# A two-layer block in one kernel: a longer stretch of one-chunk weight lookahead at the end of three matrix products

## The chip, the cores and the metric

The kernel runs on one core of a Trainium2 chip. The time is device time in microseconds (us) of one execution. A core has a matmul engine (TensorE, in the profile PE, its weight loads PEld), a vector engine (VectorE, DVE), an activation engine (ScalarE, ACT), GpSimd (POOL) and a sync engine (SP) that here only issues DMA transfers.

## The reference, cut to what matters

The input is 256 tokens of width 1024 in fp32. A first block of two layers runs, then a second one. The places of the change are in the first block:

```python
# layer 1 mixer (GLA): x @ w_in is cut into q, k, v, r, a; then a decayed state over 4 chunks of tokens
o = group_norm(o) * o_norm
m = (o * silu(r)) @ w_o                                # "gwo"
x = layer_norm(ALPHA * x + m)
x = layer_norm(ALPHA * x + conv_ffn(x))                # "up1" and "dn1"; "up0", "dn0" in layer 0
gate = sigmoid(x @ ple_w_gate[i] + ple_b_gate[i])      # "gate0" (layer 0), "gate1" (layer 1)
x = x + gate * (p[i] @ ple_w_proj[i])                  # "pa", "pb"
```

After layer 0's gate comes the GLA mixer, whose first product is "gv0". After layer 1's gate comes the second block, whose first product is "f10", a SwiGLU.

## The kernel before, in words

All weights stream from HBM in the order of use, in 556 chunks of 128x1024 fp32 (512 KB); one chunk is eight 128x128 blocks, and blocks are numbered through the whole program. Every product is done in three matmuls per block, `mm3` (lines 406 to 408): weight high half times activation high half, weight high half times activation low half, weight low half times activation high half. So each chunk has to be split before use. ScalarE writes the high half (`wh`, line 316), VectorE the low half (`wl = wraw - wh`, line 318). Both halves have eight buffers, the raw chunks six.

The class `Stream` decides where in the program these two instructions stand, and since each engine works through its instructions in program order, this is also their order in time. Whenever TensorE's code takes its first block of a new chunk c, `take` issues the preparation of further chunks: up to c + 7, but at most two at a time, when nothing else is said; up to c + 1 when `W.lazy` is 1. The low half has a rule of its own: it isn't issued with its high half but with the next chunk's preparation, or when the chunk in use is the last one prepared:

```python
la = self.lazy or min(self.LA, max(min(c, 3), c // 4))
if c >= self.np or c != self.last:
    self.prep_upto(max(c, min(c + la, self.np + 1)))
if c >= self.np - 1:
    self.flush()
```

`gemm_t` sets `W.lazy` to 1 for the last TAIL[name] blocks of a product that is called with `lazy=True` (ten where the table has no entry). The first group of a product that follows a layer norm always runs with lookahead 1, with single extra preparations (`W.fill`) at fixed steps of it. A group is two columns of blocks (four in a first group) whose results leave PSUM together.

The three products in question:

- "gate0", blocks 888 to 951, chunks 111 to 118: a first group of 32 blocks under the layer norm, then two groups of 16 blocks, chunks 115 and 116, 117 and 118. Behind each group `gate_evac` takes the sigmoid (ScalarE, line 1140), multiplies by `PP` (line 1141: VectorE, but GpSimd for columns 2 and 3) and adds to X (VectorE, line 1143). During the last group `gate_hook` splits the new X column by column into XH and XL (`xsplit`, lines 506 and 507), columns 0 to 5 before that group's steps 1 to 6. Columns 6 and 7 follow behind the last group, then a split of `ph`; then "gv0" begins with chunk 119 (its matmuls are lines 411 to 413).
- "gate1", blocks 1756 to 1819, chunks 219 to 227, built alike; "f10" follows, taking chunk 227 in its first step (lines 466 to 469) and chunk 228 in its second.
- "gwo", blocks 1148 to 1211, chunks 143 to 151: three groups of two columns, then two of one. Its evacuation (`LN.evac`, lines 571 to 595) adds each group to X and gathers the layer norm's sums, on VectorE (line 579 is the addition that frees the PSUM tile), ScalarE and GpSimd. "pa1" (one chunk of work, two groups) follows, then "up1" from block 1220, whose first group, under the layer norm, ends in chunk 156. The convolution behind each later group of "up1" is VectorE work, too (lines 1115 and 1116).

Of the kernel before, what the change touches and what calls it, by code (L numbers as in the profile page):

```python
# [144 lines left out]

TAIL = {"": 10, "gate0": 18, "gate1": 21, "aq": 24, "wo": 0, "cout": 14, "ao": 14}
LOOK = {"": 1, "aq": 2}

LN_AT = {"": (1, 2, 4), "early": (0, 1, 3)}
# [72 lines left out]
def block_kernel(ctx: ExitStack, tc: tile.TileContext, wd, xin, pin, pos, vecs, con1, con2, wa2, fb, out):  # L224
# [190 lines left out]
    def gemm_t(name, xs, T, evac, hook=None, lazy=False, ln=None, to=None, small=False, dst=None, first=False):  # L415
# [12 lines left out]
        for gi, g in enumerate(groups):  # L428
# [12 lines left out]
            for kc in range(nk):  # L441
# [4 lines left out]
                if to and base == 2 and kc == nk // 2:  # L446
                    to.mid()
                W.lazy = 1 if raw else LOOK.get(name, LOOK[""]) if lazy and W.pos >= end - TAIL.get(name, TAIL[""]) else 0
                xh, xl = ln.raw(kc) if raw else xs(kc)
# [1147 lines left out]
```

## Time and profile before

| | us |
|---|---|
| median of 3 runs | 1748.02 (1742.68 to 1754.02) |
| the profiled execution | 1743.21, of it 1741.4 span |
| TensorE busy | 1703.5 |
| VectorE busy | 1210.9 |
| ScalarE busy | 997.3 |
| GpSimd busy | 218.2 |
| mean granted TensorE clock | 0.992 |

The span is the time from the first to the last instruction of one execution. An engine's busy time is the sum of its instructions; where an instruction waited, the profile names the engine and line that released it. The granted clock is the share of full speed that TensorE was given: 1.0 or 0.5.

### The profile page before, as it was taken

The page shows a single profiled execution, that of the slowest core. Times are in us where ns is not written, and L with a number is a line of the kernel's source. Part 1 is how long each engine was busy: PE and PEld are TensorE (multiplying, and loading weights), DVE is VectorE, ACT ScalarE, POOL GpSimd, SP SyncE. Part 2 cuts the span into 40 slices and gives each one's busy share as a digit, 9 for nine tenths or more (in the row PEclk, how much of TensorE's full clock was granted, in tenths as well). Part 3 has the DMA queues.
Part 4 walks back from the last instruction along what each step waited for, and adds up shares of the span by engine and source line. Part 5 has one row for each costly group of instructions (what it writes and reads, how often), then busy time and mean ns, then how long its engine had stood idle before and what let it go on. Part 6 is the DMA issues. An engine that isn't in the chain of part 4 may idle for free.

```text
span 1741.4 us, 34304 instructions
## 1 busy us (share of the span) xinstructions
PE 1703.5 (98%) x13954; PEld 1669.3 (96%) x13954; DVE 1210.9 (70%) x1951; ACT 997.3 (57%) x1575; POOL 218.2 (13%) x244
## 2 busy tenths in 40 slices
PE   7999999999999999999999999999999999999997
PEld 6999999997899999999999999999999999999997
DVE  5777898766689986765557777556755556787553
ACT  5666766556467665654445546445555545766542
POOL 6100311020003210200002020000200001120002
PEclk9999999999999999999999999999999999999999
DMA  6445466635444665375553736554456665147651
GB/s 225 133 135 166 137 215 209 194 124 213 145 141 152 217 198 187 120 246 171 180 182 114 226 110 220 181 181 159 159 167 194 194 194 187 62 146 254 194 182 37
DMA packets 82991, 298.18 MB, mean 171 GB/s; under 512 B 9320, under 2 KB 10488, under 8 KB 82833
## 3 DMA queue, kind: packets, MB, share of 16 engines
q1 hardware_dynamic: 82176, 294.13, 52.2%
q0 software_dynamic: 656, 1.87, 0.4%
q8 instruction: 109, 1.79, 0.4%
q14 instruction: 50, 0.40, 0.1%
HBM read 294.91 MB, written 1.05 MB: 170 GB/s over the span
## 4 chain that ended last, share of the span: by engine, by line
PE 64%; DVE 3%; issue 1%; POOL 1%; ACT 0%; POOLq 0%; DVEq 0%; ACTq 0%
PE acc L406 20%; PE acc L408 20%; PE acc L407 20%; DVE wl L318 1%; DVE XL L565 0%; PE aux L645 0%; PE acc L466 0%; PE acc L469 0%; PE aux L1455 0%; PE acc L467 0%; POOL X L700 0%; PE aux L408 0%; PE aux L406 0%; PE aux L407 0%; PE aux L1478 0%
## 5 line engine op out<-in xcount | busy, mean ns | idle before, releaser
L316 ACT ACTIVATE wh<-wraw 128x1024 fp32r<-128x1024 f32 (+1 forms) x557 | 579.1, 1055 | 352.4 <-PE acc L407 297.2
L406 PE MATMUL acc<-XH,wh 128*128 128x256 f32 (+3 forms) x2660 | 749.2, 282 | 3.0 <-DVE cv L1116 2.5
L408 PE MATMUL acc<-XH,wl 128*128 128x256 f32 (+3 forms) x2660 | 746.2, 281 | 1.0 <-DVE wl L318 1.0
L407 PE MATMUL acc<-XL,wh 128*128 128x256 f32 (+3 forms) x2660 | 745.8, 280 | 0.0
L318 DVE TENSOR_TENSOR wl<-wraw,wh 128x1024 fp32r<-128x1024 f32 (+1 forms) x557 | 678.5, 1248 | 69.0 <-ACT wh L316 65.0
L406 PEld LDWEIGHTS acc<-XH,wh 128*128 128x128 f32 x2660 | 501.4, 188 | 4.1 <-ACT wh L316 1.9
L408 PEld LDWEIGHTS acc<-XH,wl 128*128 128x128 f32 x2660 | 501.1, 188 | 1.8 <-DVE wl L318 1.8
L407 PEld LDWEIGHTS acc<-XL,wh 128*128 128x128 f32 x2660 | 501.4, 188 | 0.0
L406 PE MATMUL acc<-hs,wh 128*128 128x256 f32 (+1 forms) x1044 | 292.4, 280 | 0.0
L408 PE MATMUL acc<-hs,wl 128*128 128x256 f32 (+1 forms) x1044 | 291.2, 279 | 0.0
L407 PE MATMUL acc<-hs,wh 128*128 128x256 f32 (+1 forms) x1044 | 291.2, 279 | 0.0
L407 PEld LDWEIGHTS acc<-hs,wh 128*128 128x128 f32 x1044 | 196.2, 188 | 0.2
L406 PEld LDWEIGHTS acc<-hs,wh 128*128 128x128 f32 x1044 | 196.2, 188 | 0.2
L408 PEld LDWEIGHTS acc<-hs,wl 128*128 128x128 f32 x1044 | 196.2, 188 | 0.0
L1314 DVE SCALAR_TENSOR_TENSOR sg<-acc,sg 128x272 f32<-128x272 f32 (+1 forms) x84 | 36.2, 432 | 185.3 <-ACT sg L1313 185.3
L587 POOL TENSOR_TENSOR ln_q<-ln_w 128x512 f32<-128x512 f32 (+1 forms) x10 | 14.2, 1425 | 974.5 <-ACT ln_w L581 974.5
L581 ACT ACTIVATE ln_w<-X 128x512 f32<-128x512 f32 (+3 forms) x40 | 21.3, 533 | 92.4 <-DVE X L579 92.3
L1121 POOL TENSOR_TENSOR gl<-cv,gl 128x256 f32<-128x256 f32 x44 | 39.8, 905 | 185.0 <-ACT gl L1120 105.9
L579 DVE TENSOR_TENSOR X<-acc,X 128x512 f32<-128x512 f32 (+3 forms) x40 | 22.4, 561 | 56.4 <-PE acc L408 56.2
L1313 ACT ACTIVATE sg<-acc 128x272 f32<-128x272 f32 (+1 forms) x84 | 32.5, 389 | 47.1 <-PE acc L408 46.5
L1113 ACT ACTIVATE cv<-acc,vec 128x256 f32<-128x256 f32 x80 | 40.6, 558 | 28.7 <-PE acc L408 28.6
L565 DVE SCALAR_TENSOR_TENSOR XL<-X,vec,XH 128x256 fp32r<-128x256 f32 (+1 forms) x72 | 53.9, 778 | 3.4 <-ACT XH L564 3.4
(418 smaller groups left out, 2275.8 us busy)
## 6 DMA issues: line engine op xcount, KB each, us to landing
wraw<-wd SPq DMA_DIRECT2D x555, 512.0 KB, 4.3
X<-xin SPq DMA_DIRECT2D x4, 272.0 KB, 6.2
out_t<-X SPq DMA_DIRECT2D x3, 256.0 KB, 2.7
wraw<-wd SPq DMA_DIRECT2D x2, 256.0 KB, 4.0
praw<-pin POOLq DMA_DIRECT2D x2, 256.0 KB, 3.0
fpt<-con POOLq DMA_DIRECT2D x2, 256.0 KB, 3.0
cum<-con POOLq DMA_DIRECT2D x1, 408.0 KB, 4.1
vec<-vecs SPq DMA_DIRECT2D x1, 283.0 KB, 7.6
```

The source lines that it names most:

```text
L316: A.activation(h[:, k], r[:, k], AF.Copy)
L318: self.low = lambda h=h, l=l, r=r, i=i: [V.tensor_tensor(l[:, k], r[:, k], f32(h[:, k]), op=SUB) for k in self.cuts(i)]
L406: mm(o, wh, xh, start=start, stop=False)
L407: mm(o, wh, xl, start=False, stop=False)
L408: mm(o, wl, xh, start=False, stop=stop)
L565: V.scalar_tensor_tensor(l, self.x1(m), vc(self.g, self.j + m), f32(h), op0=MUL, op1=SUB)
L579: V.tensor_tensor(xv, psum, xv, op=ADD)
L581: A.activation(sq, xv, AF.Square)
L1113: A.activation(t[:, e, :], psum[:, e, :], AF.Identity, scale=cw(2, e, j), bias=vc("cb", i * 44 + e * 22 + j))
L1121: G.tensor_tensor(gl, t[:, 0, :], gl, op=MUL)
L1313: A.activation(s, psum[:, 0, :], AF.Silu)
L1314: V.scalar_tensor_tensor(s, psum[:, 1, :], 0.5, s, op0=MUL, op1=MUL)
```

## The change

The table of tails gets an entry for "gwo" (26 blocks instead of the ten of the default), and those of "gate0" and "gate1" grow from 18 and 21 to 32 blocks, which is the whole of their last two groups. Nothing else is edited.

```diff
-TAIL = {"": 10, "gate0": 18, "gate1": 21, "aq": 24, "wo": 0, "cout": 14, "ao": 14}
+TAIL = {"": 10, "gwo": 26, "gate0": 32, "gate1": 32, "aq": 24, "wo": 0, "cout": 14, "ao": 14}
 LOOK = {"": 1, "aq": 2}
```

The number of instructions is the same; TensorE, GpSimd and SP keep their order, and on ScalarE and VectorE the two halves of some chunks move. Three places on VectorE show it. An x behind a row counts equal instructions in a row.

"gate0", from the first addition to X behind its first group to the head of "gv0"; wl is a chunk's low half. Before:

```order
L1143 TENSOR_TENSOR X<-X,sg 128x2x256
L318 TENSOR_TENSOR wl<-wraw,wh 128x1024 x2
L1143 TENSOR_TENSOR X<-X,sg 128x2x256
L318 TENSOR_TENSOR wl<-wraw,wh 128x1024 x2
L1141 TENSOR_TENSOR sg<-sg,PP 128x512
L1143 TENSOR_TENSOR X<-X,sg 128x2x256
L507 TENSOR_TENSOR XL<-X,XH 128x256 x6
L1141 TENSOR_TENSOR sg<-sg,PP 128x512
L1143 TENSOR_TENSOR X<-X,sg 128x2x256
L507 TENSOR_TENSOR XL<-X,XH 128x256 x2
L507 TENSOR_TENSOR ph<-praw,ph 128x512
L318 TENSOR_TENSOR wl<-wraw,wh 128x1024 x12
```

The same stretch with the change:

```order
L1143 TENSOR_TENSOR X<-X,sg 128x2x256 x2
L1141 TENSOR_TENSOR sg<-sg,PP 128x512
L1143 TENSOR_TENSOR X<-X,sg 128x2x256
L507 TENSOR_TENSOR XL<-X,XH 128x256 x4
L318 TENSOR_TENSOR wl<-wraw,wh 128x1024
L507 TENSOR_TENSOR XL<-X,XH 128x256 x2
L1141 TENSOR_TENSOR sg<-sg,PP 128x512
L1143 TENSOR_TENSOR X<-X,sg 128x2x256
L507 TENSOR_TENSOR XL<-X,XH 128x256 x2
L507 TENSOR_TENSOR ph<-praw,ph 128x512
L318 TENSOR_TENSOR wl<-wraw,wh 128x1024 x15
```

The four low halves of chunks 118 to 121 stood in the first of the two last groups. Now 118 stands behind four column splits of the last group, and 119, the first that "gv0" takes, behind `ph`. The high halves of chunks 119 to 122 moved likewise on ScalarE: 119 now stands behind four column splits, the others behind the whole gate.

"gate1", the same place, as a difference:

```order
 L1141 TENSOR_TENSOR sg<-sg,PP 128x512
-L1143 TENSOR_TENSOR X<-X,sg 128x2x256
-L318 TENSOR_TENSOR wl<-wraw,wh 128x1024 x2
-L1143 TENSOR_TENSOR X<-X,sg 128x2x256
+L1143 TENSOR_TENSOR X<-X,sg 128x2x256 x2
 L1141 TENSOR_TENSOR sg<-sg,PP 128x512
 L1143 TENSOR_TENSOR X<-X,sg 128x2x256
 L507 TENSOR_TENSOR XL<-X,XH 128x272 x6
+L318 TENSOR_TENSOR wl<-wraw,wh 128x1024
 L1141 TENSOR_TENSOR sg<-sg,PP 128x512
 L1143 TENSOR_TENSOR X<-X,sg 128x2x256
```

The low half of chunk 227 went behind six column splits, that of chunk 228 to the head of "f10".

"gwo", the evacuation of its third group (first addition to X) and the beginning of the fourth's:

```order
 L565 SCALAR_TENSOR_TENSOR XL<-X,vec,XH 128x256 x2
-L318 TENSOR_TENSOR wl<-wraw,wh 128x1024 x2
+L318 TENSOR_TENSOR wl<-wraw,wh 128x1024
 L579 TENSOR_TENSOR X<-acc,X 128x2x256
 L586 TENSOR_TENSOR ln_d<-ln_d,X 128x2x256
 L591 TENSOR_TENSOR ln_d<-ln_d 128x256
 L565 SCALAR_TENSOR_TENSOR XL<-X,vec,XH 128x256 x2
-L318 TENSOR_TENSOR wl<-wraw,wh 128x1024
 L579 TENSOR_TENSOR X<-acc,X 128x256
 L594 TENSOR_TENSOR ln_d<-ln_d,X 128x256
```

Two of three low halves left "gwo". The rows of the low halves up to the third group of "up1" stay where they are, but each now holds a chunk two lower; the two that are missing are made up for behind that program's second convolution (four in a row instead of two).

## Rows read from the trace of the kernel before

**Rows 1.** The page, first part: busy us, share of the span, instructions.

```profile
PE 1703.5 (98%) x13954; PEld 1669.3 (96%) x13954; DVE 1210.9 (70%) x1951; ACT 997.3 (57%) x1575; POOL 218.2 (13%) x244
```

**Rows 2.** The page, costliest groups: busy us, mean ns | idle before, releaser.

```profile
L316 ACT ACTIVATE wh<-wraw 128x1024 fp32r<-128x1024 f32 (+1 forms) x557 | 579.1, 1055 | 352.4 <-PE acc L407 297.2
...
L318 DVE TENSOR_TENSOR wl<-wraw,wh 128x1024 fp32r<-128x1024 f32 (+1 forms) x557 | 678.5, 1248 | 69.0 <-ACT wh L316 65.0
```

**Rows 3.** Timeline of TensorE, "gate0" into "gv0": start, us, instruction [idle before].

```profile
394.17 0.38 PE L408 MATMUL acc<-XH,wl 128*128 128x256 f32 x1 [0.54 <-DVE wl L318]
...
396.81 0.42 PE L411 MATMUL acc<-wh,XH 128*128 128x512 f32 x1
...
399.85 0.50 PE L413 MATMUL acc<-wh,XL 128*128 128x512 f32 x1 [2.38 <-DVE XL L507]
```

**Rows 4.** Timelines of GpSimd and ScalarE, end of "gate0".

```profile
391.30 1.74 POOL L1141 TENSOR_TENSOR sg<-sg,PP 128x512 f32<-128x512 f32 x1 [4.76 <-ACT sg L1140]
...
400.18 0.82 ACT L1140 ACTIVATE sg<-acc,vec 128x256 f32<-128x256 f32 x2
```

**Rows 5.** Timeline of VectorE, end of "gate0".

```profile
391.79 3.46 DVE L318 TENSOR_TENSOR wl<-wraw,wh 128x1024 fp32r<-128x1024 f32 x2
...
395.78 2.34 DVE L318 TENSOR_TENSOR wl<-wraw,wh 128x1024 fp32r<-128x1024 f32 x2
398.05 0.68 DVE L1141 TENSOR_TENSOR sg<-sg,PP 128x512 f32<-128x512 f32 x1
398.76 0.69 DVE L1143 TENSOR_TENSOR X<-X,sg 128x512 f32<-128x512 f32 x1
399.37 2.09 DVE L507 TENSOR_TENSOR XL<-X,XH 128x256 fp32r<-128x256 f32 x6
...
404.78 9.41 DVE L318 TENSOR_TENSOR wl<-wraw,wh 128x1024 fp32r<-128x1024 f32 x8
```

**Rows 6.** Table by stretch: busy us by engine, granted clock, DMA share, GB/s.

```profile
397.00:400.00 3.00, 0.62 (x3) 0.16 (x3) 2.97 (x5) 0.45 (x2) 0.00 (x0) 1.00 0.93 270
...
515.00:522.00 7.00, 7.00 (x36) 7.00 (x35) 2.98 (x11) 2.77 (x6) 0.18 (x1) 0.51 0.12 26
...
734.00:737.00 3.00, 3.00 (x15) 3.00 (x15) 2.41 (x6) 1.48 (x3) 0.00 (x0) 0.52 0.02 8
```

**Rows 7.** Timeline of VectorE, end of "gate1" into "f10".

```profile
726.59 3.47 DVE L318 TENSOR_TENSOR wl<-wraw,wh 128x1024 fp32r<-128x1024 f32 x2
...
731.90 2.19 DVE L507 TENSOR_TENSOR XL<-X,XH 128x272 fp32r<-128x272 f32 x6
...
736.69 8.03 DVE L318 TENSOR_TENSOR wl<-wraw,wh 128x1024 fp32r<-128x1024 f32 x7
```

**Rows 8.** Timelines of ScalarE and TensorE, same place.

```profile
732.74 0.82 ACT L1140 ACTIVATE sg<-acc,vec 128x256 f32<-128x256 f32 x2
...
733.61 0.60 PE L466 MATMUL acc<-XH,wh 128*128 128x272 f32 x1 [2.70 <-ACT sg L1140]
```

**Rows 9.** Timelines of TensorE ("pa1", second group) and VectorE ("gwo").

```profile
514.53 0.36 PE L406 MATMUL acc<-ph,wh 128*128 128x256 f32 x1 [2.97 <-DVE X L579]
...
504.67 2.35 DVE L318 TENSOR_TENSOR wl<-wraw,wh 128x1024 fp32r<-128x1024 f32 x2
...
511.06 1.21 DVE L318 TENSOR_TENSOR wl<-wraw,wh 128x1024 fp32r<-128x1024 f32 x1
...
513.96 0.42 DVE L579 TENSOR_TENSOR X<-acc,X 128x256 f32<-128x256 f32 x1
```

**Rows 10.** Timeline of VectorE, "up1".

```profile
534.76 1.22 DVE L318 TENSOR_TENSOR wl<-wraw,wh 128x1024 fp32r<-128x1024 f32 x1
...
538.29 1.22 DVE L318 TENSOR_TENSOR wl<-wraw,wh 128x1024 fp32r<-128x1024 f32 x1
...
543.46 5.18 DVE L318 TENSOR_TENSOR wl<-wraw,wh 128x1024 fp32r<-128x1024 f32 x4
```

**Rows 11.** Timeline of TensorE, "up1": chunk 157's first low-half matmul; fifth group's first.

```profile
533.64 0.28 PE L408 MATMUL acc<-XH,wl 128*128 128x256 f32 x1
...
550.61 0.36 PE L406 MATMUL acc<-XH,wh 128*128 128x256 f32 x1 [1.71 <-DVE cv L1116]
```

## The prediction, made before the changed kernel ran

> **What bounds the kernel now.** I read the page's first part, then the waits by engine, then timelines of the three places that the change touches. TensorE is busy 98% of the span [rows 1], so a change to the order of preparations can only move the waits left on TensorE and the stretches at half clock that follow them. A weight chunk costs ScalarE 1.05 us and VectorE 1.25 us [rows 2], beside 2.7 us of TensorE; in the long run ScalarE waits for buffers that TensorE frees (297.2 of 352.4 us idle) [rows 2], so lookahead is full there and worth nothing. It is worth something where evacuation and preparation meet on VectorE, and the change moves it exactly there. Four rows show the price today: TensorE waits 0.54 us for a low half in the middle of "gate0", 2.38 us at the head of "gv0" for an XL split [rows 3], 2.70 us at the head of "f10" [rows 8] and 2.97 us in "pa1" for the last addition to X of "gwo" [rows 9]. The table by stretch adds the clock: 0.51 for the 7 us behind the wait of 2.97, 0.52 for 3 us behind that of 2.70, but 1.00 in the wait of 2.38 [rows 6].
>
> **gate0: the loss.** Four low halves leave VectorE between the evacuations of the gate's first and second group, and four high halves leave ScalarE there. They were early for chunks 119 to 121, but not for 118, whose low half now stands behind the second group's evacuation and four column splits. When it gets done: GpSimd's product ends at 391.30 + 1.74 = 393.04 [rows 4]; VectorE then does one addition to X (0.61, start to start of 398.76 and 399.37), product and addition of the second group (1.32), four splits (4 of the 2.09 for six, 1.39) and the low half (1.17, half of 2.34) [rows 5]: 397.5. TensorE got it at 394.1 and had waited 0.54 [rows 3]; now it waits 3.9, a delay of 3.4. That ScalarE is free 3.9 us earlier helps nobody here, since VectorE waits for GpSimd.
>
> VectorE's first low half of the pair at 391.79 took its share of 3.46 us where a pair takes 2.34 [rows 5]: it stood still until GpSimd's product was done, so that product does not end sooner now that the pair is gone. The Trainium skill (SBUF — State Buffer, section "SBUF: two separate sides") says the port pair of the two engines is an exclusive lock; by it 393.04 stands as I use it, and if they slowed each other instead, both gates would come out some 0.5 us better.
>
> Chunk 118 then runs from 397.5 as before from 394.17 to 396.81 [rows 3], to 400.2. Chunk 119's low half now stands behind the last group's sigmoid, product, addition, two splits and `ph`. Before, from that sigmoid's start (400.18) to the next low half (404.78) went 4.60 [rows 4, 5]; 0.4 of it was VectorE still splitting (399.37 + 2.09 = 401.46 against a sigmoid done at 401.00). So 400.2 + 4.2 + 1.17 = 405.6, and only then can "gv0" do its second matmul, where before its third started at 399.85 [rows 3]. With 0.23 for the one matmul between: **+5.9 us**, the wait of 2.38 already credited. TensorE idles 3.9 and then 5.2 us, both longer than any wait in these rows. If each drops the clock, chunk 118 takes 2.5 longer and the head of "gv0" loses 3.4 (49% of 7 us) [rows 6]: bounds 5.4 to 11.8. I take 5.9 and half of the two clock terms, since of the three nearest waits two cost clock and these for 3 and 7 us: **+8.9**.
>
> **gate1: the same, milder.** The pair at 726.59 took 3.47 instead of 2.34 [rows 7], so GpSimd held VectorE until 727.7. Behind it now come addition 0.61, product and addition 1.32, six splits 2.19 [rows 7], then chunk 227's low half 1.17: 733.0. TensorE wants it in the gate's last four blocks; the gate ended near 730.6 (the head of "f10" was ready at 733.61 - 2.70 = 730.9 after two matmuls) [rows 8], so at 729.4: a wait of 3.6. The rest of the gate ends at 734.2, the last sigmoid starts there instead of at 732.74 [rows 8]. From it to the low half of the head of "f10" at 736.69 went 3.95 [rows 7], 0.5 of it VectorE's late splits: 734.2 + 3.45 + 1.17 = 738.8 for chunk 228, needed in the second step of "f10", which before reached that point 12 matmuls behind 733.61, at half clock 0.227 each, 736.3. So **+2.5**, and with half rate in the last four blocks (1.1) and behind the wait (1.6 to 3.4) up to 7.0; low 2.0. I take 2.5 and half of 1.1 and 1.6: **+3.9**.
>
> **gwo: a gain that "up1" takes back.** Two low halves leave VectorE ahead of the addition that frees the tile for "pa1" (one of the pair at 504.67, and the one at 511.06; 1.13 each): the wait shrinks from 2.97 to 0.7, by 2.3 [rows 9], and no wait of 1.71 or 2.38 cost clock here [rows 11, 6], so the 7 us at 0.51 go as well, 3.4: -5.7 for TensorE, and for the layer norm's chain on VectorE, which starts from TensorE's sums. But "up1" now starts two chunks poorer: the rows of its low halves keep their places and hold chunks two lower. Taken in the old frame of time: chunk 157's low half is the row at 534.76, done 535.9 [rows 10], wanted at 533.64 [rows 11]: 2.25 late. Chunk 158 is wanted 2.7 later, 538.6, done 539.4: 0.8 late. Chunk 159, first of the four at 543.46, is wanted at 542.1, done 544.6: 2.5 late. Together 5.6. Against that goes the fifth group's wait at 550.61 (1.71 and the 0.2 of drain before it) [rows 11], which is covered now: +3.7. The two low halves that follow later (2.3) delay the evacuation that the sixth group waits for, by then with some 2 us to spare. Net **-2.0**; bounds -5.7 (these chunks are in time) and +1.4 (one of the waits drops the clock, 3.4).
>
> **Other queues.** SP and GpSimd keep their order; a chunk's transfer is issued with the preparation five chunks ahead of it and moves along. Five raw chunks wait at each place, and at 270 GB/s [rows 6] one more comes every 1.9 us, faster than TensorE's 2.7: nothing for that, but in "up1" eight preparations nearly in a row may find the transfers late by 2 to 3 us; the same 2 us cover it.
>
> **Sum.** 8.9 + 3.9 - 2.0 = +10.8. On the profiled execution (1743.21, span 1741.4 and 1.8 around it) that is 1754.0; it lies 4.8 below the median of the three runs, 1748.02, so on the median **1759**.
>
> **The rivals.**
> - *The clock holds* (chance 0.20): +5.9 + 2.5 - 2.0 = +6.4, 1754. For it: the wait of 2.38 with clock 1.00 [rows 6]. Against: longer waits.
> - *Slower by over 1%* (0.17): every long wait is followed by half rate. Gate0 11.8, gate1 7.0, and in "up1" the waits for chunks 157 and 159 drop the clock too, +1.4: +20.2, 1768. It decides if TensorE's clock reads 0.5 at three places: behind chunk 118's wait, at the head of "gv0" and within "up1". For it: [rows 6], two of three. The Trainium skill (TensorE: Matmul & The Clock Gate, section "HAM oscillation — how this bites in real kernels") says that a loop of short bursts between long waits starts each burst at half rate; that is this case, and it speaks against the change. Whether the bursts here are of that kind no row shows.
> - *Faster* (0.06): the gates' evacuation is earlier by the removed casts and the low halves come in time anyway: waits of 0.54, 2.38 and 2.70 go, -5.6, and "gwo" keeps -5.7: 1737. Against: the order of instructions puts both low halves behind the evacuation.
> - *The change does nothing* (0.02): the names in the table aren't those asked for. The order moved, so no; 1748.
>
> The forecast has 0.55, with a range of its own of 1753 to 1765.
>
> **Range and chances.** From 1749 (the gate terms' low ends with most of the "gwo" gain) to 1769 (the slow rival, and 1 us for the runs' spread); left out are the faster rival, and the upper part of the slow one, some 0.2. One per cent, about what can be told from no change, is 17.5 us: faster by more 0.01, within 0.81, slower by more 0.18 (most of the slow rival and a tail of the forecast).
>
> **What would show it.** On TensorE: a wait for a low half (line 318) of 3 to 4 us inside the last group of "gate0", one of 5 at the second matmul of "gv0", the wait for XL gone; one of 3 to 4 in the last group of "gate1", one of 2 or more in the second step of "f10"; "pa1" waits under 1, no half clock behind it, then three waits for low halves in the second and third group of "up1", and none at the fifth. Wrong it is if TensorE's waits for line 318 in both gates stay under 1 us, or if "up1" runs without them.

## The result, and the profile after

| | before | changed |
|---|---|---|
| median of 6 runs each, us | 1746.85 (1742.68 to 1754.02) | 1760.84 (1757.52 to 1766.20) |
| profiled execution, us | 1743.21 (span 1741.4) | 1766.20 (span 1764.4) |
| mean granted clock in it | 0.992 | 0.984 |

The ratio is 1.0083, 95% interval 1.0066 to 1.0100: slower by 14.0 us, 11.5 to 17.5. The forecast was 1759 within 1749 to 1769, a loss of 10.8. The profiled execution of the changed kernel is the longest of its six, so the two spans, 23.0 apart, are not the result; which part of the 23.0 belongs to the change is read from the places.

The page's first part answers to [rows 1]: busy us, share of the span, instructions.

```profile
PE 1717.3 (97%) x13954; PEld 1682.2 (95%) x13954; DVE 1205.9 (68%) x1951; ACT 998.6 (57%) x1575; POOL 217.7 (12%) x244
```

As many instructions as before; VectorE has less busy time and TensorE 13.8 more, for a matmul at half clock is busy for longer. Next, TensorE's waits over the whole program, grouped (engine, tile and line, released by; us in total, times, longest):

```profile
PE acc L408 <- DVE wl L318: 14.5, 8, 4.2
...
PE acc L412 <- DVE wl L318: 5.2, 1, 5.2
...
PE acc L406 <- DVE X L579: 0.9, 2, 0.7
PE acc L406 <- DVE cv L1116: 0.8, 1, 0.8
```

A low half of a weight chunk (`wl`, line 318) now holds TensorE for 19.7 us; the wait of "pa1" for the addition to X is 0.7 instead of 2.97 [rows 9], and the wait for XL at the head of "gv0" [rows 3] is no longer in the list. The wait of 1.71 at the fifth group of "up1" [rows 11] is gone, too: the 0.8 in the last row stands at 215.9 us, in layer 0, where the kernel before has it as well. Where the 19.7 lie, but for a wait of 0.27 in "up1", the timeline of TensorE shows: "gate0" and "gv0" (the fourth row is the first small matmul behind "gv0"), "pa1", "up1" (its last row here is the fifth group's first matmul, with no wait), "gate1" and the second step of "f10".

```profile
390.67 0.39 PE L408 MATMUL acc<-XH,wl 128*128 128x256 f32 x1 [0.49 <-DVE wl L318]
...
397.69 0.58 PE L408 MATMUL acc<-XH,wl 128*128 128x256 f32 x1 [3.98 <-DVE wl L318]
...
408.39 0.80 PE L412 MATMUL acc<-wl,XH 128*128 128x512 f32 x1 [5.21 <-DVE wl L318]
...
421.67 0.28 PE L406 MATMUL aux<-XH,wh 128*16 128x256 f32 x1
...
523.24 0.35 PE L406 MATMUL acc<-ph,wh 128*128 128x256 f32 x1 [0.70 <-DVE X L579]
...
541.45 0.38 PE L408 MATMUL acc<-XH,wl 128*128 128x256 f32 x1 [1.57 <-DVE wl L318]
...
544.99 0.39 PE L408 MATMUL acc<-XH,wl 128*128 128x256 f32 x1 [0.50 <-DVE wl L318]
...
550.14 0.39 PE L408 MATMUL acc<-XH,wl 128*128 128x256 f32 x1 [2.12 <-DVE wl L318]
...
559.59 0.28 PE L406 MATMUL acc<-XH,wh 128*128 128x256 f32 x1
...
742.01 0.58 PE L408 MATMUL acc<-XH,wl 128*128 128x256 f32 x1 [4.17 <-DVE wl L318]
...
749.44 0.39 PE L408 MATMUL acc<-XH,wl 128*128 128x272 f32 x1 [1.40 <-DVE wl L318]
```

Before, the first and the fourth of these matmuls stood here:

```profile
390.60 0.39 PE L408 MATMUL acc<-XH,wl 128*128 128x256 f32 x1 [0.45 <-DVE wl L318]
...
410.69 0.28 PE L406 MATMUL aux<-XH,wh 128*16 128x256 f32 x1
```

20.09 us from one to the other before, 31.00 now: **+10.9 in "gate0" and "gv0"**. The same subtraction between equal matmuls gives **-2.1** from "gwo" to behind the fifth group of "up1" (50.90 to 48.77) and **+4.3** from "gate1" into "f10" (22.92 to 27.18). Together 13.1, near the 14.0 of the medians. The stretches between the three places are alike to 0.05 (94.36 and 94.36 from "gv0" to "gwo", 166.08 and 166.08 from "up1" to "gate1"). The other 10 of the 23.0 come later than the change, in "f20" and at three places where the clock fell (the last section).

VectorE's timeline shows what stands ahead of those low halves; GpSimd's one row, last, is its product in "gate0".

```profile
393.14 0.69 DVE L1143 TENSOR_TENSOR X<-X,sg 128x512 f32<-128x512 f32 x1 [1.20 <-POOL sg L1141]
...
396.42 1.22 DVE L318 TENSOR_TENSOR wl<-wraw,wh 128x1024 fp32r<-128x1024 f32 x1
...
403.73 0.69 DVE L1141 TENSOR_TENSOR sg<-sg,PP 128x512 f32<-128x512 f32 x1 [2.62 <-ACT sg L1140]
...
407.12 9.16 DVE L318 TENSOR_TENSOR wl<-wraw,wh 128x1024 fp32r<-128x1024 f32 x8
...
740.75 1.21 DVE L318 TENSOR_TENSOR wl<-wraw,wh 128x1024 fp32r<-128x1024 f32 x1
...
391.38 1.73 POOL L1141 TENSOR_TENSOR sg<-sg,PP 128x512 f32<-128x512 f32 x1 [4.77 <-ACT sg L1140]
```

The place where two low halves used to stand is now idle time (1.20), because GpSimd's product takes 1.73 without the pair beside it as it took 1.74 with it [rows 4]. Chunk 118's low half then ends at 397.64 and TensorE starts at 397.69. VectorE stands idle for 2.62 until the last sigmoid is there, with the low half of chunk 119 not yet issued: in program order it comes behind that sigmoid's product, its addition, two column splits and the split of `ph`.

The table by stretch has the clock in the column ahead of the DMA share:

```profile
397.00:403.00 6.00, 5.31 (x23) 4.98 (x23) 1.49 (x3) 0.98 (x3) 0.00 (x0) 0.50 0.29 90
...
408.00:413.00 5.00, 4.61 (x11) 3.68 (x12) 5.00 (x6) 4.27 (x5) 0.00 (x0) 0.50 0.69 202
...
520.00:530.00 10.00, 9.30 (x80) 9.14 (x79) 6.46 (x19) 5.72 (x11) 2.51 (x4) 1.00 0.14 50
...
741.00:748.00 7.00, 5.90 (x24) 5.40 (x24) 2.88 (x5) 1.85 (x5) 0.00 (x0) 0.51 0.21 75
```

Behind all three waits of about 4 and 5 us TensorE works at half clock, and behind "pa1", where it was 0.51 [rows 6], it is at 1.00.

### The profile page after: what moved, and what is told of

The parts are those of the page before. It is cut to its first block, busy times and chain, and to the rows that moved or that the text cites. A ratio compares the mean times of both kernels' runs of the same rounds, so it can differ in the third digit from the quotient of the medians.

```text
span 1764.4 us, 34300 instructions
## 1 busy us (share of the span) xinstructions
PE 1717.3 (97%) x13954; PEld 1682.2 (95%) x13954; DVE 1205.9 (68%) x1951; ACT 998.6 (57%) x1575; POOL 217.7 (12%) x244
## 4 chain that ended last, share of the span: by engine, by line
PE 64%; DVE 3%; POOL 1%; issue 1%; ACT 0%; POOLq 0%; DVEq 0%; ACTq 0%
PE acc L406 20%; PE acc L408 20%; PE acc L407 20%; DVE wl L318 1%; PE aux L645 1%; POOL X L700 1%; DVE XL L565 0%; PE acc L469 0%; PE acc L466 0%; PE aux L1455 0%; PE acc L467 0%; PE aux L408 0%; PE aux L406 0%; PE aux L407 0%; PE aux L1478 0%
```

## The experiments

All were timed in five rounds against the kernel before on the same chip (three chips in all, so experiments are compared with each other by their ratios); a difference of 0.1% is 1.75 us.

**1. Each of the three numbers alone.**

```diff
-TAIL = {"": 10, "gate0": 18, "gate1": 21, ...
+TAIL = {"": 10, "gwo": 26, "gate0": 18, "gate1": 21, ...     (gwo only)
+TAIL = {"": 10, "gate0": 32, "gate1": 21, ...                (gate0 only)
+TAIL = {"": 10, "gate0": 18, "gate1": 32, ...                (gate1 only)
```

> Only gwo gets its 26 blocks; both gates keep 18 and 21. Theory (a gain that up1 takes back): TensorE's wait in pa1 falls from 2.97 to about 0.7 us and the half clock behind it goes (-5.7 us), then three or four waits for low halves in up1 give back about 3.7: net -2 us, ratio 0.999. Rival (the lower lookahead costs nothing in up1, the whole loss of the change is the gates'): no waits for low halves in up1, -5.7 us, ratio 0.9967.

> Only gate0 gets its 32 blocks. Theory: TensorE waits 4.0 us for chunk 118's low half and 5.2 us for chunk 119's, both followed by half clock: +11 us, ratio 1.0063, with +5.9 of it waits and the rest clock. Rival (gate0 and gate1 cost the same, their work being alike): about +6.7, half of what the two gates cost together.

> Only gate1 gets its 32 blocks. Theory: waits of 3.6 to 4.2 us for chunk 227's low half and about 1.4 for chunk 228's in f10's second step, half clock in between, the old wait of 2.7 gone: +4.4 us, ratio 1.0025. Rival as for gate0: +6.7.

| | ratio (95%) | us | same stretch in its trace |
|---|---|---|---|
| gwo only | 1.0000 (0.9989 to 1.0012) | 0.0 | -0.6 |
| gate0 only | 1.0053 (1.0037 to 1.0070) | +9.3 | +11.0 |
| gate1 only | 1.0024 (1.0010 to 1.0038) | +4.2 | +6.0 |

The parts add up: 13.5 against 14.0 for all three. "gate0" makes two thirds of the loss and "gwo" makes nothing, since what it gives in "pa1" goes back in "up1". The rival of gwo only (0.9967) lies outside the interval. That of the gates, 6.7 us (1.0038) for each, lies at the edge of both intervals; the traces, 11.0 and 6.0, speak against it. A single trace is not the median, though: in that of gate1 only, the clock made two stretches that its edit doesn't touch differ from before, by +1.5 in "gate0" and "gv0" and by -1.8 from "gwo" to the fifth group of "up1". In the trace of gwo only, TensorE is 5.4 us ahead behind "pa1" and its stretch at half clock, and 0.6 ahead behind the fifth group of "up1"; the largest of the three waits in between dropped the clock in this execution (0.57 us for a matmul that takes 0.39 at full clock):

```profile
538.99 0.57 PE L408 MATMUL acc<-XH,wl 128*128 128x256 f32 x1 [2.16 <-DVE wl L318]
```

**2. gate0 only, with TensorE kept busy in its two waits.** What does the clock cost there? Matmuls on constants, whose result nobody reads, fill the wait for chunk 118 and the wait at the second matmul of "gv0"; nothing else differs from gate0 only. First 14 and 20 of them:

```diff
+    def busy(n):
+        t = aux()
+        for _ in range(n):
+            mm(t[:, :NT], cst("c256", P), con[:, :NT], start=True, stop=True)
...
+            if i == 0 and (gi, kc) == (2, 4):
+                busy(14)
...
+           lambda kc, b: (kc, b) == (0, 0) and busy(20))
```

> As the run with gate0 alone, but TensorE gets 14 dummy matmuls (128x256, fp32, own PSUM tile, result unused) right before the block at which it waits for chunk 118's low half, and 20 before gv0's first matmul, so that it computes while it waits. Theory (half of gate0's price is the clock): no half clock in gate0 and at the head of gv0, the waits themselves stay covered by dummies, +6 us instead of +11, ratio 1.0034. Rival (the price is the late low halves alone, the clock is incidental): +11 as without dummies, or more by what dummies take.

Measured 1.0065 (1.0048 to 1.0082), which settles nothing: one such product is two matmuls of 0.22 us, twice what I had reckoned, so the filling outlasted the waits by over 1 and some 3 us. Then 11 and 12:

> The same as the run before with dummies, but with 11 and 12 of them instead of 14 and 20, since one took 0.415 us there and the two rows outlasted the waits by 1 and 3 us. Theory (half of gate0's price is the clock): no half clock in gate0 and gv0's head, TensorE reaches gv0's second low-half product 6 us later than before and not 11, ratio about 1.003. Rival (the clock is incidental): 1.0053 as with gate0 alone.

Measured 1.0038 (1.0022 to 1.0053), 2.6 us less than gate0 only. The two intervals overlap, and the rival's 1.0053 is at the end of this one, so the clock's share is read from the traces. The timeline of TensorE (the line numbers of its rows behind 404 are higher by five; the rows named `aux<-con` are the filling):

```profile
391.07 0.38 PE L413 MATMUL acc<-XH,wl 128*128 128x256 f32 x1 [0.47 <-DVE wl L318]
...
393.72 4.91 PE L408 MATMUL aux<-con 128*128 128x256 f32 x22
398.28 0.47 PE L411 MATMUL acc<-XH,wh 128*128 128x256 f32 x1
...
398.71 0.28 PE L413 MATMUL acc<-XH,wl 128*128 128x256 f32 x1
...
401.20 5.34 PE L408 MATMUL aux<-con 128*128 128x256 f32 x24
...
407.00 0.50 PE L417 MATMUL acc<-wl,XH 128*128 128x512 f32 x1 [0.23 <-DVE wl L318]
...
418.07 0.28 PE L411 MATMUL aux<-XH,wh 128*16 128x256 f32 x1
```

and its table by stretch:

```profile
398.00:401.00 3.00, 3.00 (x26) 2.92 (x26) 0.89 (x3) 0.84 (x2) 0.00 (x0) 1.00 0.50 175
401.00:406.00 5.00, 5.00 (x27) 4.43 (x26) 3.03 (x6) 2.99 (x7) 1.38 (x3) 1.00 0.06 13
406.00:413.00 7.00, 6.77 (x30) 5.18 (x29) 7.00 (x7) 5.42 (x7) 0.00 (x0) 1.00 0.63 205
```

The low half of chunk 118 was done at 398.03. In the changed kernel the first matmul that takes it starts 0.05 behind that; here the filling and two matmuls of the chunk stand ahead of it, and it starts at 398.71, 0.6 late. Some 0.1 of this comes back, since the first matmul behind a wait costs that much more (0.23 us to the next one instead of 0.12): by this estimate the first filling is 0.5 too long. The second is a little short. From 391.07 to 418.07 are 27.0, without the 0.5 26.5: the waits alone cost 26.5 - 20.1 = **6.4** us, and with the clock at half the stretch took 31.1 in gate0 only (31.0 in the changed kernel): the clock adds **4.6**. Two other ways come to the same. In gate0 only, chunk 118's matmuls took 2.2 us more than at full clock, and from the second matmul of "gv0" to the first small matmul behind it went 13.4 instead of the 11.1 here, 2.3 more. And the run with 14 and 20, whose fillings were 1.8 and 3.0 too long, gives 6.4 for the waits, too. The half clock is gone where TensorE is kept busy, so its share is shown by a run; its size is good to some tenths of a us, from one execution of each kernel.

**3. The changed kernel with the next chunk's low half ahead of the evacuation.** Is it the place of the low half behind the evacuation, or the shorter lookahead as such? The flush issues a prepared chunk's low half at the end of a group, ahead of its evacuation on VectorE.

```diff
                 W.fill(F[1])
+                if name in ("gate0", "gate1"):
+                    W.flush()
```

> The change, with one line more: behind the first group of both gates the pending low half is issued at once (chunk 118 in gate0, 227 in gate1), so it stands ahead of the evacuation; the number of prepared chunks is as in the change. Theory (it is the place of the low half behind the evacuation, not the number of chunks ahead): the waits of 4 us inside both gates go; those at gv0's head (chunk 119) and in f10 (chunk 228) stay. gate0 +6 instead of +11, gate1 +1 instead of +4.4, ratio about 1.0035. Rival (two chunks too few are what costs, wherever the low half stands): 1.008 as in the change.

Measured 1.0018 (1.0003 to 1.0033), from 1.0083, with the same lookahead of one chunk. TensorE's timeline, at the head of "gv0" and in "f10":

```profile
402.10 0.80 PE L412 MATMUL acc<-wl,XH 128*128 128x512 f32 x1 [5.58 <-DVE wl L318]
...
735.20 0.39 PE L466 MATMUL acc<-XH,wh 128*128 128x272 f32 x1 [2.75 <-ACT sg L1142]
...
739.13 0.59 PE L408 MATMUL acc<-XH,wl 128*128 128x272 f32 x1 [2.43 <-DVE wl L318]
```

The waits for chunks 118 and 227 are gone, and those for the chunks behind them, which the flush doesn't reach, are there (5.58 and 2.43). The stretches cost 4.6 and 2.9 instead of 10.9 and 4.3, where I expected 6 and 1, and the ratio came out lower than the theory's 1.0035. The rival's 1.008 is out: most of the loss was the order on VectorE.

**4. "gate0" in small steps.** With 24 blocks one pair of low halves fewer stands on VectorE ahead of the second group's evacuation; with 14, one pair more stands ahead of the six column splits.

```diff
-TAIL = {"": 10, "gate0": 18, ...
+TAIL = {"": 10, "gate0": 24, ...                 (gate0 24)
+TAIL = {"": 10, "gwo": 26, "gate0": 14, ...      (gate0 14, with the W.fill(2) of experiment 5)
+TAIL = {"": 10, "gwo": 26, "gate0": 24, ...      (gate0 24, with the W.fill(2) of experiment 5)
```

> gate0 with 24 blocks instead of 18, the rest as before: chunks 119 and 120 are prepared in the second group as before, 121 and 122 behind the gate; low halves of 118 and 119 keep their places. Theory (only 118 and 119 are needed early, the other two delay the XL split that gv0 waits for): TensorE's 2.4 us wait at gv0 falls to under 0.5, nothing new: -2.2 us, ratio 0.9987. Rival (any chunk fewer ahead costs): +2 us or more at gv0, ratio 1.001.

> The other direction: gwo 26 with two chunks prepared behind its product (0.9970 by itself), and gate0 14 instead of 18, so that two low halves stand on VectorE ahead of the six column splits of the second group. Theory (at this place a low half costs TensorE whatever stands behind it on VectorE): the wait for XL at the head of gv0 grows from 2.4 by 2.3 to 4.7 us, nothing else waits for a low half there; by itself 0.9983, and 1.0003 if the longer wait drops the clock for 6.8 us. Rival (more lookahead pays, since chunks 118 to 121 are ready sooner): 0.995 to 0.9975, with the waits of 0.5 in gate0 gone.

> gwo 26 with two chunks prepared behind its product, and gate0 24 instead of 18; gate1 as before. The version without the gate0 part measured 0.9970. In the trace of gate0 24 alone, gate0 into gv0 took 24.03 us from the second chunk's wait to the first of the small matmuls, against 20.09 before, 3.94 more; but the median of its runs was that of before (0.9995). Theory (the 3.94 is a real cost): 0.9970 + 0.0022 = 0.999 (0.9977 to 1.0005). Rival (gate0 24 is free, the 3.94 belongs to that one execution): 0.9967 (0.995 to 0.9977).

Gate0 24 measured 0.9995 (0.9981 to 1.0009). The wait of 2.38 for XL at the head of "gv0" went, as the theory had it, but "nothing new" was wrong: TensorE gets through chunk 119 and waits 3.37 at the fourteenth matmul of "gv0", the first that takes the low half of chunk 120, which now stands behind `ph`. So chunk 120 is needed early, too. Half clock follows: +3.9 us in that execution, which the medians don't show. Together with experiment 5 the same number measured 0.9990 (0.9978 to 1.0003), where experiment 5 alone has 0.9970. The same wait in both traces, first alone (with the XL product that no longer waits ahead of it), then with experiment 5, each followed by its row of the table by stretch:

```profile
396.63 0.50 PE L413 MATMUL acc<-wh,XL 128*128 128x512 f32 x1
...
402.83 0.79 PE L412 MATMUL acc<-wl,XH 128*128 128x512 f32 x1 [3.37 <-DVE wl L318]
...
403.00:409.00 6.00, 6.00 (x15) 4.67 (x16) 6.00 (x6) 4.41 (x5) 0.00 (x0) 0.54 0.82 258
```

```profile
402.55 0.50 PE L412 MATMUL acc<-wl,XH 128*128 128x512 f32 x1 [3.36 <-DVE wl L318]
...
403.00:409.00 6.00, 6.00 (x28) 4.80 (x27) 6.00 (x6) 4.13 (x5) 0.00 (x0) 1.00 0.82 264
```

Equal waits of 3.37 and 3.36 us, and clocks of 0.54 and 1.00: the stretch costs 3.9 in one and 1.4 in the other. The ratio of the run with both is the theory's 0.999, and the rival's range (up to 0.9977) ends below its interval; but that run's own trace has 1.4 and not 3.9, so all that can be said is that 24 costs between 0 and some 3 us.

Gate0 14 measured 0.9986 (0.9970 to 1.0001), between the theory's two numbers (0.9983 without a fall of the clock, 1.0003 with one) and not better than experiment 5's 0.9970. The waits of 0.5 that the rival wanted gone are there (0.48 and 0.54). Its head of "gv0":

```profile
400.27 0.50 PE L411 MATMUL acc<-wh,XH 128*128 128x512 f32 x1 [3.68 <-ACT XH L506]
...
401.73 0.80 PE L413 MATMUL acc<-wh,XL 128*128 128x512 f32 x1 [0.73 <-DVE XL L507]
```

I expected the wait of 2.38 for XL to grow to 4.7. It came to 4.41, in two pieces, and the first is for XH, which ScalarE writes behind its own two added casts; the second of these had itself waited 2.55 us for the transfer of its chunk. The second piece is the low halves on VectorE, and behind it the clock fell (0.80 us for a matmul that takes 0.50 at full clock behind a wait). In this trace the stretch took 3.8 us longer than before, so more lookahead costs here, too. That 18 is better than 14 and 24 is shown by these traces; by the medians neither is clear of experiment 5, since the intervals overlap.

**5. gwo only, with two chunks prepared right behind its product.** If "up1" takes the gain back because it starts two chunks short, giving them back between the last addition of "gwo" and "up1" must keep it.

```diff
     gemm_t("gwo", ..., lazy=True, to=ln)
+    W.fill(2)
```

> gwo with its 26 blocks and both gates as before, and two chunks are prepared right behind gwo's last group, ahead of pa1, so that up1 starts with the chunks it had before. Theory (up1 takes the gain back because it starts two chunks poorer): pa1's wait 0.7 us and no half clock, no wait for low halves in up1, the wait of 1.7 at up1's fifth group back: -5 us, ratio 0.997. Rival (the two preparations cost in the layer norm what they save in gwo): 1.000 as with gwo alone.

Measured **0.9970 (0.9955 to 0.9984), 1742.14 against 1747.41**: 5.3 us faster than the kernel before, and the best of all that ran. Its waits:

```profile
PE acc L406 <- DVE cv L1116: 2.4, 2, 1.7
...
PE acc L408 <- DVE wl L318: 1.4, 3, 0.5
...
PE acc L406 <- DVE X L579: 0.9, 2, 0.7
```

No wait for a low half above 0.5; the one at the fifth group of "up1" is back at 1.7, the one in "pa1" stays at 0.7. From "gwo" to behind that fifth group it is 4.7 us shorter than before.

## Why the prediction was right, and by how much its terms were off

- **gate0, +8.9 forecast, +10.9 in the trace, +9.3 by the runs of that number alone.** The waits came as worked out: 3.9 and 5.2 forecast, 3.98 and 5.21 measured, and the wait for XL went. The wait part is 6.4 (experiment 2) instead of 5.9. The missing 0.5 is in small pieces of the sum: from the end of chunk 118's matmuls to the start of the second matmul of "gv0" I had 5.4 and it took 5.8 (TensorE's drain ahead of the last sigmoid was left out), and chunk 118 began 0.1 later than my 397.5. The clock part is 4.6 where I took 3.0, half of 5.9. It fell behind both waits, and the two falls cost 2.2 and 2.3 where my bounds were 2.5 and 3.4: the half was wrong, and bounds that were too high hid part of it. My reason for a half was three waits in the rows of before, two with and one without a fall, and those were of 2.4 to 3.0 us.
- **gate1, +3.9 forecast, +4.3 in the trace, +4.2 alone.** The wait for chunk 227 was 4.17 (3.6 forecast: its low half was done as forecast, but TensorE wanted it at 729.0 and not at 729.4), that for chunk 228 1.40 (2 or more forecast): the later chunk has the shorter wait, since TensorE came to it later, at half clock.
- **gwo, -2.0 forecast, -2.1 in the trace, 0.0 alone (-1.9 to +2.1).** Both steps are there: 0.7 in "pa1" and full clock behind it, then 1.57, 0.50 and 2.12 in "up1" where I had 2.25, 0.8 and 2.5, and the fifth group's wait is covered. In us of TensorE's timeline that is 5.4 gained, 5.3 given back and 2.0 covered, where I had 5.7, 5.6 and 1.9. The interval of gwo only ends just short of that sum; in its own trace, where the clock fell at 538.99, the stretch is only 0.6 shorter. I had the five raw chunks and the transfers as harmless, and no wait for a transfer appeared among those of TensorE.
- **The sum**, 10.8, lies just below the interval of the measured difference (11.5 to 17.5). The term that was mis-sized is the clock at "gate0" and "gv0", and with it the small pieces of the wait: 2.0 of the 2.3 between 10.8 and the 13.1 at the three places. That the time itself, 1760.84, is only 1.8 above 1759 is luck in part: the median before, with six runs, is 1.2 below the 1748.02 that the forecast was added to.
- **The lock between VectorE and GpSimd** was used to keep 393.04 for the end of the product. It ended at 393.11, 1.73 long with no pair beside it.
- **The rivals.** The clock held nowhere behind the long waits, so 1754 was out. The slow rival asked for half clock at three places, "up1" among them; there it held in the changed kernel and fell in gwo only (0.57 us at 538.99). The fast rival failed where I said: the program order puts the low halves behind the evacuation, and moving them (experiment 3) gives most of the loss back.

What stays open: why the same wait of 3.4 us at the same place drops the clock in one execution and not in another. Experiment 4 shows that it does, not on what it hangs. The row on which the half rested is of this kind. The wait of 2.38 at the head of "gv0" kept the clock at 1.00 in the traces of before, of gwo only and of experiment 5, and dropped it in that of gate1 only:

```profile
400.27 0.71 PE L413 MATMUL acc<-wh,XL 128*128 128x512 f32 x1 [2.38 <-DVE XL L507]
```

The two waits that had cost clock in the rows of before did so again in every trace that has them: about 2.97 in six traces, about 2.70 in nine.

## What to carry to other kernels

Reducing lookahead to get evacuations done sooner moves work, it does not remove it: ask where the skipped preparation stands in its engine's program order instead, and what stands ahead of it there. Here it went behind a chain of evacuations that ends in a wait for TensorE itself, and in "gate0" that cost 6.4 us of waits and 4.6 of clock; in "gwo" it was worth 5 us once the two skipped chunks were made up for at once, behind the addition that had to come first. Where TensorE is busy 98% of the span, price each new wait of 4 us with the half clock behind it: all seven waits of 3.97 to 5.58 us in these traces had it.

## What the runs showed of the hardware that was not expected

The same run of matmuls has two rates at full clock. In the long products of the second block ("f10", "f20"), 128x272 matmuls with no wait and clock 1.00, a stretch of 100 us held 813 of them in one trace and 792 in another; which of the products is slow differs from trace to trace (gate1 only has the slow rate in "f10", the changed kernel and gate0 14 in "f20"; experiment 3, which has all three numbers of the change, has it in neither). On what it hangs is open, with one trace of each kernel. The rows are those of "f20", before and in the changed kernel:

```profile
1060.00:1160.00 100.00, 100.00 (x813) 100.00 (x812) 57.68 (x74) 51.32 (x75) 0.00 (x0) 1.00 0.64 204
```

```profile
1075.00:1175.00 100.00, 100.00 (x792) 100.00 (x791) 57.45 (x74) 49.83 (x72) 0.00 (x0) 1.00 0.61 197
```

That is 123 and 126 ns per matmul, and 3.8 us over that product. With the clock's falls at places that the change doesn't touch (near 1044, 1311 and 1567 in the changed kernel's trace; before, only the first of them, and shorter), this makes the difference between 14.0 by the medians and 23.0 by the two profiled executions. A single profile of this kernel is good for the place of a wait, not for its effect on the total.
